# Down-projection of a hybrid layer: weight and product blocks prepared three steps ahead instead of two

## The chip, the cores and the metric

The kernel runs on one core of one Trainium2 chip. The core has a matrix engine (TensorE, PE in the profile; its weight loads are PEld), VectorE (DVE), ScalarE (ACT), GpSimd (POOL), SyncE (SP, used here to issue transfers) and 16 DMA engines. Each engine runs its own instructions in the order in which they stand; between engines, semaphores order the work. The metric is the device time of one execution in microseconds (us); lower is better.

## The reference, cut to what matters

The program is one layer of a streaming encoder: a gated recurrent branch and an attention branch, merged, and then a feed-forward part with a causal convolution. The change lies in the last matrix product, the down-projection.

```python
# x: (1, 512, 1024), D_FF = 3072
...
    h = rms_norm(x, ffn_norm_pre[layer])
    up = jnp.einsum("bsd,df->bsf", h, w_up[layer])
    up = causal_dwconv(up, conv_f_w[layer], conv_f_b[layer])
    gate, val = jnp.split(up, 2, axis=-1)
    ffn_out = jnp.einsum("bsf,fd->bsd", jax.nn.gelu(gate) * val, w_down[layer])
    x = x + rms_norm(ffn_out, ffn_norm_post[layer])
```

Below, y is `gelu(gate) * val` (512 x 3072) and W the matrix `w_down` (3072 x 1024).

## The kernel before

**Seven products in 42 steps.** y is halved by tokens and by the contraction, W by the contraction and by output columns, and the product is formed by Strassen's scheme in Winograd's form: seven products of 256 tokens x 1536 x 512 columns instead of eight, in the order `PRODUCTS = (1, 4, 5, 6, 7, 3, 2)`. Each product runs over six blocks of 256 rows of W, and one block of one product is a step: steps 0 to 5 are product 1, 6 to 11 product 4, 12 to 17 product 5, 18 to 23 product 6, 24 to 29 product 7, 30 to 35 product 3, 36 to 41 product 2. The sums of the parts of W that products 4 to 7 need were formed in DRAM much earlier (the tiles `td`).

**Three matmuls for one.** Every float32 operand is split into a rounded high part and the rest: `Split.hi` (L205, ScalarE) writes `wh` from the fetched `raw` weights, `Split.lo` (L208, VectorE) writes `wl = raw - wh`. `y_hi` (L1461, ScalarE) and `y_lo` (L357, VectorE) do the same with a block of y, into `ah` and `al`. `down_step(i)` then issues twelve matmuls (L1495 to L1497: high by high, high by low, low by high, for two token tiles and two halves of the block). `prep(i)` issues the four splitting instructions of step i, in the order wh, ah (ScalarE), wl, al (VectorE). `load_w(i)` issues the fetch of `raw` on SyncE's queue.

**Buffers.** `raw`, `wh` and `wl` have four buffers each. `ah` and `al` have three for the first six steps and four from step 6 on. A buffer is written again when its last reader is done, and the program's semaphores see to that.

**The order** in this part is that in which the code is written; no scheduler moves it. The loop over steps i from 3 on issued: the fetch of the weights of step i + 5, the matmuls of step i, `prep(i + 2)`, and then a list `extra[i]` of other work:

- loads of blocks of y from DRAM into tiles `q` (L1569, SyncE): the blocks of product 4 in `extra[4..6]`, of product 5 in `extra[6..11]`, of products 6 and 7 in `extra[12..17]`, of products 3 and 2 in `extra[19..24]`, and the gain `gpost` in `extra[5]`
- combinations of such blocks on VectorE (L357 and L1572 with `q` on both sides), which make the blocks of products 5, 6, 7 and 3: the one that makes the block of step j stands in `extra[j - 4]`, for steps 12 to 35
- "holds" on ScalarE (L1600), two copies each that save a sum out of its PSUM bank: product 1 in `extra[6]`, product 4 in `extra[12]`, product 5 in `extra[18]`, and products 1 + 6 in `extra[23]`. Products 6 and 7 are added onto the bank of product 1, so step 24 writes into a bank that the last of these holds reads
- in `extra[9]` the negation of half of the gain and the load of another activation table (L1645, L1646, ScalarE)
- from `extra[30]` on folds of sums into the held ones (L1603, VectorE), multiplications by the gain (L1613, VectorE), sums of squares (L1610, ScalarE), and, in `extra[34]` and `extra[38]`, the root of the mean square of an output tile (L1619 and L272 on VectorE, L270 on ScalarE) with its scaling (L1629, ScalarE)

The last four steps (`LATE`) are issued after the loop, token tile by token tile, so that the first tile of outputs is complete early; the second is formed in two halves of 256 columns. Then come the last folds (L1688), the last root and the outputs.

Of the kernel before, what the change touches and what calls it, by code (L numbers as in the profile page):

```python
# [97 lines left out]
def kernel(  # L98
# [55 lines left out]
    def down_block(i, c, m):  # L154
        return w_down[(2 * i + c) * NS + m]
# [859 lines left out]
    with ExitStack() as at:  # L1015
# [141 lines left out]
        i = KD - 2  # L1157
# [287 lines left out]
    STEPS = [(n, m) for n in PRODUCTS for m in range(NS)]  # L1445
    wd, yraw, yhl, dpools, LATE = {}, {}, {}, [], 4

    def load_w(i):
        if i < len(STEPS):
            n, m = STEPS[i]  # L1450
            wd[i] = Split(td[WQ[n]][m] if n > 3 else down_block(*WQ[n], m), (2, DH), f"dn{n}_{m}")
# [5 lines left out]
    def y_hi(i):  # L1457
        pl, b = (ypool, 3) if i < NS else (dpools[0], LATE)
        yhl[i] = [pl.tile([P, 2, SH], F32R, tag=f"a{x}", name=f"a{x}{i}", bufs=b) for x in "hl"]
        yhl[i].append(yraw[STEPS[i]])  # L1460
        act.copy(yhl[i][0], yhl[i][2])  # L1461

    def y_lo(i):
        sub(yhl[i][1], yhl[i][2], yhl[i][0].bitcast(F32))

    def prep(i):
        if i < len(STEPS):
            wd[i].hi()
            y_hi(i)
            wd[i].lo(dve)  # L1470
            y_lo(i)
# [3 lines left out]
    def down_step(i, ts=(0, 1), c=None):  # L1475
        n, m = STEPS[i]
        fresh = n in (1, 2, 4, 5)
        if m == 0 and fresh and ts[0] == 0:
            slot[n] = [bank(f"dn{n}_{t}") for t in range(2)]
            if n == 2:  # L1480
                slot[n][1] = [slot[n][1], bank("dn2_2")]
        dst = slot[{6: 1, 7: 1, 3: 5}.get(n, n)]
        wh, wl = wd[i].parts()
        ah, al = yhl[i][:2]
        for t in ts:
            tok = slice(P * t, P * (t + 1))
            outs = [(dst[t], slice(0, DH))]
            if isinstance(dst[t], list):
                outs = [(dst[t][h], x) for h, x in enumerate((X, Y)) if c in (None, x)]
            for d, x in outs:  # L1490
                h = slice(x.start // 2, x.stop // 2)
                for k in range(2):
                    first, last = fresh and m == k == 0, m == NS - 1 and k == 1
                    bh, bl = turns(wh[:, k], SH)[:, h], turns(wl[:, k], SH)[:, h]
                    pe.matmul(d[:, x], ah[:, k, tok], bh, start=first, stop=False, skip_group_check=True)  # L1495
                    pe.matmul(d[:, x], ah[:, k, tok], bl, start=False, stop=False, skip_group_check=True)  # L1496
                    pe.matmul(d[:, x], al[:, k, tok], bh, start=False, stop=last, skip_group_check=True)  # L1497
# [13 lines left out]
    with man2:  # L1511
# [152 lines left out]
            extra[a].append(lambda t=t: (square(t, 1, kept[6][t]), gained(t, 1, kept[6][t])))  # L1664

        for i in range(3, len(STEPS)):
            load_w(i + 5)
            if i < len(STEPS) - LATE:
                down_step(i)
            if i < len(STEPS) - LATE:  # L1670
                prep(i + 2)
                for f in extra[i]:
                    f()
        for i in range(len(STEPS) - LATE, len(STEPS)):
            prep(i + 2)
        for i in range(len(STEPS) - LATE, len(STEPS)):
            for f in extra[i]:
                f()
# [117 lines left out]
```

## Time and profile before

| what | time |
|---|---|
| three runs, median (lowest to highest) | 883.2 us (882.61 to 883.78) |
| the profiled execution's own time | 883.07 us |
| its span, first to last instruction | 881.3 us |
| busy in the span: TensorE, VectorE, ScalarE, GpSimd | 867.8, 738.7, 600.1, 235.8 us |
| first matmul of step 0, last matmul | 760.87, 873.27 us |

The span is shorter than the execution's own time because start and end of the program lie around it. Busy times overlap between engines, so they don't add up. A row of a timeline gives the start and the length of an instruction in us, its engine and line, what it writes and reads, and in brackets how long the engine stood idle before it and what ended that. A row of the waits view gives an engine's line, what it waited for, and the total, the number and the longest of these waits. Starts count from the span's start, and an engine may start an instruction a little before the one before it has ended.

### The profile page before, as it was taken

Reading aid. Unit: us, or ns where it says so; the run is one execution under the profiler, and the core shown is the slowest. Engines: PE = TensorE matmul, PEld = TensorE weight load, DVE = VectorE, ACT = ScalarE, POOL = GpSimd, SP = SyncE. Lnnn points to the kernel's source line nnn. Section 1 sums busy time; section 2 is a strip of 40 time slices with the busy share of each in tenths; the row PEclk is TensorE's granted clock in tenths of the full one; section 3 lists DMA queues with packets and bytes.
Section 4 is the critical chain, followed back from the end, with each engine's and each line's share of the span. In section 5 each row is a group of like instructions: output and inputs, shape, how many; then the busy total and the mean of one; then the engine's idle time right before and its main releaser. Section 6 shows DMA issues by size and latency. Waiting matters only on the chain.

```text
span 881.3 us, 15793 instructions
## 1 busy us (share of the span) xinstructions
PE 867.8 (98%) x5856; PEld 792.9 (90%) x5856; DVE 738.7 (84%) x1209; ACT 600.1 (68%) x1031; POOL 235.8 (27%) x283
## 2 busy tenths in 40 slices
PE   9999999999999999999999999999999999999996
PEld 7888888888899998888888889999999999988885
DVE  8986479738878849998968698999999999889897
ACT  7565695533466648786755487878888888677664
POOL 4244334535411024223204100233233333100000
PEclk9999999999999999999999999999999999999998
DMA  7788689999864478344506663689999998699875
GB/s 269 235 264 234 193 195 267 250 270 189 193 176 140 120 259 276 136 164 136 203 26 201 221 203 105 147 207 248 257 239 249 235 215 215 221 388 349 296 204 156
DMA packets 71968, 188.38 MB, mean 214 GB/s; under 512 B 7313, under 2 KB 27841, under 8 KB 71506
## 3 DMA queue, kind: packets, MB, share of 16 engines
q1 hardware_dynamic: 48288, 130.86, 44.7%
q0 software_dynamic: 23456, 56.37, 29.7%
q8 instruction: 46, 0.75, 0.3%
q14 instruction: 32, 0.26, 0.1%
q10 hardware_dynamic: 146, 0.14, 0.1%
HBM read 152.79 MB, written 37.83 MB: 216 GB/s over the span
## 4 chain that ended last, share of the span: by engine, by line
PE 82%; DVE 8%; issue 4%; ACT 2%; POOL 2%; DMA 1%; DVEq 0%; SPq 0%; ACTq 0%; POOLq 0%
PE up L462 7%; PE up L464 7%; PE up L461 7%; PE dn L1497 2%; PE ga L252 2%; PE ga L251 2%; PE ga L253 2%; PE dn L1496 2%; PE dn L1495 2%; PE pb L251 2%; PE xa L251 2%; PE v L341 2%; PE xa L253 2%; PE v L342 2%; PE v L343 2%
## 5 line engine op out<-in xcount | busy, mean ns | idle before, releaser
L397 POOL DMA_DIRECT2D ml<-raw_up x42 | 36.1, 860 | 149.6 <-ACT ml L396 84.2
L1370 DVE SCALAR_TENSOR_TENSOR u<-up,cpt,u 128x511 f32<-128x511 f32 x96 | 71.3, 745 | 3.5 <-ACT u L1364 1.8
L1497 PE MATMUL dn<-wh_dn,al 128*128 128x512 f32 (+1 forms) x180 | 66.2, 368 | 0.4
L1496 PE MATMUL dn<-wl_dn,ah 128*128 128x512 f32 (+1 forms) x180 | 65.9, 366 | 0.0
L1495 PE MATMUL dn<-wh_dn,ah 128*128 128x512 f32 (+1 forms) x180 | 65.7, 365 | 0.0
L461 PE MATMUL up<-sh,th 128*128 128x256 f32 x252 | 59.5, 275 | 0.0
L462 PE MATMUL up<-sl,th 128*128 128x256 f32 x252 | 59.5, 275 | 0.0
L208 DVE TENSOR_TENSOR wl_dn<-raw_dn,wh_dn 128x1024 fp32r<-128x1024 f32 x42 | 51.2, 1220 | 7.3 <-ACT wh_dn L205 7.3
L205 ACT CAST wh_dn<-raw_dn 128x1024 fp32r<-128x1024 f32 x42 | 44.0, 1049 | 15.6 <-PE dn L1497 8.3
L357 DVE TENSOR_TENSOR tl<-t,th 128x1024 fp32r<-128x1024 f32 x42 | 51.1, 1217 | 0.0
L1364 ACT ACTIVATE u<-up,cpt 128x512 f32<-128x512 f32 x48 | 36.9, 777 | 20.1 <-PE up L464 10.0
L461 PEld LDWEIGHTS up<-sh,th 128*128 128x128 f32 x252 | 48.4, 192 | 0.0
L462 PEld LDWEIGHTS up<-sl,th 128*128 128x128 f32 x252 | 48.4, 192 | 0.0
L1378 POOL TENSOR_TENSOR yf<-u,u 128x512 f32<-128x512 f32 x23 | 30.5, 1325 | 57.6 <-issue 44.7
L443 ACT CAST th<-t 128x1024 fp32r<-128x1024 f32 x42 | 43.7, 1044 | 2.4
L1497 PEld LDWEIGHTS dn<-wh_dn,al 128*128 128x128 f32 x180 | 34.1, 189 | 6.3 <-DVE al L357 2.2
L461 PE MATMUL up<-h2h,mh 128*128 128x256 f32 x168 | 39.7, 275 | 0.0
L462 PE MATMUL up<-h2l,mh 128*128 128x256 f32 x168 | 39.7, 275 | 0.0
L1050 ACT ACTIVATE P<-P,mx 128x384 f32<-128x384 f32 (+3 forms) x64 | 35.2, 552 | 5.6 <-DVE mx L1045 4.6
L955 POOL TENSOR_TENSOR B<-B,mask 128x128 f32<-128x128 f32 x64 | 29.4, 488 | 34.8 <-DMA B<-cnd 34.7
L464 PE MATMUL up<-sh,tl 128*128 128x256 f32 x252 | 38.4, 275 | 0.0
L1496 PEld LDWEIGHTS dn<-wl_dn,ah 128*128 128x128 f32 x180 | 34.1, 189 | 4.7 <-DVE wl_dn L208 0.6
(731 smaller groups left out, 3234.6 us busy)
## 6 DMA issues: line engine op xcount, KB each, us to landing
raw_up<-in_w_up_dram SPq DMA_DIRECT2D x48, 512.0 KB, 5.6
td<-in_w_down_dram POOLq DMA_DIRECT2D x36, 512.0 KB, 6.6
raw_dn<-td SPq DMA_DIRECT2D x24, 512.0 KB, 5.3
ml<-raw_up POOLq DMA_DIRECT2D x21, 512.0 KB, 5.4
B<-cnd POOLq DMA_DIRECT2D x16, 640.0 KB, 5.7
raw_dn<-in_w_down_dram SPq DMA_DIRECT2D x18, 512.0 KB, 4.0
raw_wo<-in_w_out_dram SPq DMA_DIRECT2D x16, 512.0 KB, 4.3
td<-td POOLq DMA_DIRECT2D x12, 512.0 KB, 11.7
```

What stands on the lines that cost most here:

```text
L205: act.copy(self.wh, self.raw)
L208: engine.tensor_tensor(out=self.wl, in0=self.raw, in1=self.wh.bitcast(F32), op=ALU.subtract)
L251: pe.matmul(dst, ah, bh, start=first, stop=False)
L357: dve.tensor_tensor(out=out, in0=a, in1=b, op=ALU.subtract)
L443: act.copy(self.th[i], self.t[i])
L461: pe.matmul(dst, wh[:, k], turns(ah[:, k]), start=first and k == 0, stop=False, skip_group_check=True)
L462: pe.matmul(dst, wh[:, k], turns(al[:, k]), start=False, stop=False, skip_group_check=True)
L464: pe.matmul(dst, wl[:, k], turns(ah[:, k]), start=False, stop=k == KH - 1, skip_group_check=True)
L1370: dve.scalar_tensor_tensor(out=c[:, s:], in0=ps[:, : S - s], scalar=col(C_CFW + 3 * e + j), in1=c[:, s:], op0=ALU.mult, op1=ALU.add)
L1495: pe.matmul(d[:, x], ah[:, k, tok], bh, start=first, stop=False, skip_group_check=True)
L1496: pe.matmul(d[:, x], ah[:, k, tok], bl, start=False, stop=False, skip_group_check=True)
L1497: pe.matmul(d[:, x], al[:, k, tok], bh, start=False, stop=last, skip_group_check=True)
```

## The change

The preparation behind step i is that of step i + 3, and the fetch that of step i + 6. The preparation of step 5 and the fetch of step 8 are issued ahead of step 3. Buffers, instructions and the lists `extra` stay as they were, and the loop behind the steps issues what is left.

```diff
         for i in range(3, len(STEPS)):
-            load_w(i + 5)
+            if i == 3:
+                prep(5)
+                load_w(8)
+            load_w(i + 6)
             if i < len(STEPS) - LATE:
                 down_step(i)
-            if i < len(STEPS) - LATE:
-                prep(i + 2)
+                prep(i + 3)
                 for f in extra[i]:
                     f()
         for i in range(len(STEPS) - LATE, len(STEPS)):
-            prep(i + 2)
+            prep(i + 3)
```

How the engines' orders change is shown at three places. In the rows, `wh_dn6_5` is the rounded weight tile of block 5 of product 6 (step 23), `ah25` the rounded product block of step 25, `q11_1` the loaded or combined block that it is made from; the number at the end of a name counts buffers.

ScalarE around the hold of products 1 + 6, before:

```order
L205 CAST wh_dn6_5_9965<-raw_dn6_5_9964 128x1024
L1461 CAST ah23_10059<-q00_5_9962 128x512
L205 CAST wh_dn7_0_9993<-raw_dn7_0_9992 128x1024
L1461 CAST ah24_10084<-q11_0_9569 128x512
L205 CAST wh_dn7_1_10018<-raw_dn7_1_10017 128x1024
L1461 CAST ah25_10109<-q11_1_9571 128x512
L1600 COPY kept6_0_10117<-dn1_0_9452 128x512
L1600 COPY kept6_1_10118<-dn1_1_9453 128x512
L205 CAST wh_dn7_2_10043<-raw_dn7_2_10042 128x1024
L1461 CAST ah26_10138<-q11_2_9573 128x512
```

and now:

```order
L205 CAST wh_dn6_5_9950<-raw_dn6_5_9949 128x1024
L1461 CAST ah23_10044<-q00_5_9972 128x512
L205 CAST wh_dn7_0_9975<-raw_dn7_0_9974 128x1024
L1461 CAST ah24_10069<-q11_0_9569 128x512
L205 CAST wh_dn7_1_10003<-raw_dn7_1_10002 128x1024
L1461 CAST ah25_10094<-q11_1_9571 128x512
L205 CAST wh_dn7_2_10028<-raw_dn7_2_10027 128x1024
L1461 CAST ah26_10119<-q11_2_9573 128x512
L1600 COPY kept6_0_10127<-dn1_0_9452 128x512
L1600 COPY kept6_1_10128<-dn1_1_9453 128x512
```

The two copies of the hold moved behind the casts of step 26. The same happened to the other holds and to the gain.

VectorE at the same place, before (L1572 writes the block of a later step, `q11_2` that of step 26):

```order
L208 TENSOR_TENSOR wl_dn7_0_9994<-raw_dn7_0_9992,wh_dn7_0_9993 128x1024
L357 TENSOR_TENSOR al24_10085<-q11_0_9569,ah24_10084 128x512
L1572 SCALAR_TENSOR_TENSOR q11_2_9573<-q00_2_9887,q11_2_9573 128x512
L208 TENSOR_TENSOR wl_dn7_1_10019<-raw_dn7_1_10017,wh_dn7_1_10018 128x1024
L357 TENSOR_TENSOR al25_10110<-q11_1_9571,ah25_10109 128x512
L1572 SCALAR_TENSOR_TENSOR q11_3_9623<-q00_3_9912,q11_3_9623 128x512
L208 TENSOR_TENSOR wl_dn7_2_10044<-raw_dn7_2_10042,wh_dn7_2_10043 128x1024
```

and now:

```order
L208 TENSOR_TENSOR wl_dn7_0_9976<-raw_dn7_0_9974,wh_dn7_0_9975 128x1024
L357 TENSOR_TENSOR al24_10070<-q11_0_9569,ah24_10069 128x512
L1572 SCALAR_TENSOR_TENSOR q11_1_9571<-q00_1_9871,q11_1_9571 128x512
L208 TENSOR_TENSOR wl_dn7_1_10004<-raw_dn7_1_10002,wh_dn7_1_10003 128x1024
L357 TENSOR_TENSOR al25_10095<-q11_1_9571,ah25_10094 128x512
L1572 SCALAR_TENSOR_TENSOR q11_2_9573<-q00_2_9897,q11_2_9573 128x512
L208 TENSOR_TENSOR wl_dn7_2_10029<-raw_dn7_2_10027,wh_dn7_2_10028 128x1024
```

The combination that makes the block of step 26 stood ahead of the weights of step 25 and stands now right ahead of those of step 26.

SyncE, which issues the transfers, from the fetch of the weights of step 9 (`raw_dn4_3`) on, before:

```order
L199 DMA raw_dn4_3_9601<-td3_3_114 128x1024
L1569 DMA q11_3_9623<-yd9_6583 128x2x256
L199 DMA raw_dn4_4_9625<-td3_4_115 128x1024
L1569 DMA q11_4_9647<-yd10_6584 128x2x256
L1644 DMA gpost_9568<-in_gains_dram 128x1024
L199 DMA raw_dn4_5_9650<-td3_5_116 128x1024
L1569 DMA q10_0_9674<-yd0_6574 128x2x256
L1569 DMA q11_5_9676<-yd11_6585 128x2x256
L199 DMA raw_dn5_0_9682<-td0_0_93 128x1024
```

and now:

```order
L199 DMA raw_dn4_3_9589<-td3_3_114 128x1024
L199 DMA raw_dn4_4_9611<-td3_4_115 128x1024
L1569 DMA q11_3_9633<-yd9_6583 128x2x256
L199 DMA raw_dn4_5_9635<-td3_5_116 128x1024
L1569 DMA q11_4_9657<-yd10_6584 128x2x256
L1644 DMA gpost_9568<-in_gains_dram 128x1024
L199 DMA raw_dn5_0_9660<-td0_0_93 128x1024
L1569 DMA q10_0_9684<-yd0_6574 128x2x256
L1569 DMA q11_5_9686<-yd11_6585 128x2x256
```

Each load of a product block moved behind one more fetch of weights: the block of step 11 (`q11_5`) stood ahead of the weights of step 12 (`raw_dn5_0`) and stands now behind them.

## The prediction

> **What bounds the kernel now.** I read the page first (span, chain), then the windows of the last 110 us, then each engine's timeline there. I call the 42 steps of the down-projection 0 to 41; "weights j" and "block j" are the weight and product block of step j, wh/ah their rounded and wl/al their remaining parts.
>
> ```profile
> span 881.3 us, 15793 instructions
> PE 82%; DVE 8%; issue 4%; ACT 2%; POOL 2%; DMA 1%; DVEq 0%; SPq 0%; ACTq 0%; POOLq 0%
> 820.00:825.00 5.00, 5.00 (x25) 4.38 (x24) 4.88 (x7) 2.16 (x3) 0.00 (x0) 1.00 1.03 356
> 870.00:875.00 5.00, 3.55 (x32) 3.35 (x31) 4.43 (x11) 2.08 (x8) 0.00 (x1) 1.00 0.61 105
> 875.00:881.30 6.30, 0.00 (x0) 0.00 (x0) 2.26 (x6) 0.65 (x3) 0.00 (x0) 0.61 0.67 250
> PEld dn L1497 <- DVE al L357: 2.2, 5, 0.5
> PEld dn L1496 <- DVE wl_dn L208: 0.6, 2, 0.4
> ```
>
> The first number of a windows row is the stretch, then the busy time of PE, PEld, DVE, ACT, POOL, the granted clock, the DMA share and GB/s. TensorE is never idle from 820 to 825, and all its waits of the whole stage come to 2.2 + 0.6 = 2.8 us, always for VectorE's subtractions. So a deeper preparation could win at most 2.8 us while TensorE stays the bound.
>
> ```profile
> 822.46 1.22 DVE L208 TENSOR_TENSOR wl_dn<-raw_dn,wh_dn 128x1024 fp32r<-128x1024 f32 x1
> 823.60 0.68 DVE L357 TENSOR_TENSOR al<-q,ah 128x512 fp32r<-128x512 f32 x1
> 824.20 0.68 DVE L1572 SCALAR_TENSOR_TENSOR q<-q,q 128x512 f32<-128x512 f32 x1
> 827.14 1.22 DVE L208 TENSOR_TENSOR wl_dn<-raw_dn,wh_dn 128x1024 fp32r<-128x1024 f32 x1 [2.26 <-ACT wh_dn L205]
> ...
> 844.12 1.22 DVE L208 TENSOR_TENSOR wl_dn<-raw_dn,wh_dn 128x1024 fp32r<-128x1024 f32 x1
> ...
> 853.47 0.22 DVE L1619 TENSOR_SCALAR ss_o<-s_o 128x1 f32<-128x1 f32 x1
> ...
> 856.42 1.23 DVE L208 TENSOR_TENSOR wl_dn<-raw_dn,wh_dn 128x1024 fp32r<-128x1024 f32 x1 [1.62 <-ACT wh_dn L205]
> ...
> 865.18 1.22 DVE L208 TENSOR_TENSOR wl_dn<-raw_dn,wh_dn 128x1024 fp32r<-128x1024 f32 x1
> ...
> 874.40 0.42 DVE L1688 TENSOR_TENSOR kept<-dn,kept 128x256 f32<-128x256 f32 x1
> ```
>
> These are wl25, al25, one combination of product blocks (call it s), wl26, wl33, the sum of squares of output tile 2, wl37, wl41, and the last fold. A step costs VectorE 1.14 (wl to al) + 0.60 (al to s) + 0.60 (s to wl) = 2.34 us.
>
> ```profile
> 825.37 0.38 PE L1495 MATMUL dn<-wh_dn,ah 128*128 128x512 f32 x1
> ...
> 827.96 0.38 PE L1495 MATMUL dn<-wh_dn,ah 128*128 128x512 f32 x1
> ...
> 873.27 0.28 PE L1497 MATMUL dn<-wh_dn,al 128*128 128x256 f32 x1
> ```
>
> Steps 24 and 25 begin here: a step is 2.59 us on TensorE. VectorE is thus a little faster than TensorE until folds join it; the sums of the last token half end at 873.27 + 0.28 = 873.55, but their fold starts at 874.40, because VectorE is behind. **The end hangs on VectorE**, which from wl37 (856.42) on stops only for three short square-root round trips.
>
> **The change part by part.** (a) No instruction is added or removed. The waits are on the same buffers: four of each weight tile, so wh of step j may be written when step j-4 has run, and raw weights j are fetched when wl of step j-4 is done. The preparation of step 5 ahead of step 3, and the late loop, leave ScalarE's and VectorE's order as it was: 0 us. What moves is what stands between the preparations, shown in the rows of the change: holds, the gain's scaling, the combinations s and the loads of product blocks all come one preparation later.
>
> (b) SyncE: block loads now stand behind one more weight load.
>
> ```profile
> 777.08 0.32 SPq L199 DMA_DIRECT2D raw_dn<-td  x1
> 777.45 0.53 SPq L1569 DMA_DIRECT2D q<-yd  x1
> ...
> 781.04 0.32 SPq L199 DMA_DIRECT2D raw_dn<-td  x1
> ...
> raw_dn<-td SPq DMA_DIRECT2D x24, 512.0 KB, 5.3
> raw_dn<-in_w_down_dram SPq DMA_DIRECT2D x18, 512.0 KB, 4.0
> 780.00:785.00 5.00, 4.99 (x23) 4.07 (x22) 4.65 (x6) 5.00 (x8) 0.00 (x0) 1.00 1.05 397
> ```
>
> ```profile
> 780.18 1.05 ACT L205 CAST wh_dn<-raw_dn 128x1024 fp32r<-128x1024 f32 x1
> 781.13 0.62 ACT L1461 CAST ah<-q 128x512 fp32r<-128x512 f32 x1
> 781.65 1.06 ACT L1600 COPY kept<-dn 128x512 f32<-128x512 f32 x2
> 782.61 1.06 ACT L205 CAST wh_dn<-raw_dn 128x1024 fp32r<-128x1024 f32 x1
> ...
> 786.95 1.04 ACT L205 CAST wh_dn<-raw_dn 128x1024 fp32r<-128x1024 f32 x1 [1.30 <-DMA raw_dn<-td]
> 788.41 0.62 ACT L1461 CAST ah<-q 128x512 fp32r<-128x512 f32 x1 [0.42 <-DMA q<-yd]
> 788.94 0.62 ACT L1645 ACTIVATE gpost<-gpost 128x512 f32<-128x512 f32 x1
> ...
> 790.98 1.03 ACT L205 CAST wh_dn<-raw_dn 128x1024 fp32r<-128x1024 f32 x1
> ...
> 803.91 0.62 ACT L1461 CAST ah<-q 128x512 fp32r<-128x512 f32 x1 [0.26 <-DVE q L1572]
> ...
> 820.44 1.06 ACT L205 CAST wh_dn<-raw_dn 128x1024 fp32r<-128x1024 f32 x1 [1.01 <-PE dn L1497]
> ...
> 824.28 0.59 ACT L1600 COPY kept<-dn 128x512 f32<-128x512 f32 x1 [2.27 <-PE dn L1497]
> 825.57 0.59 ACT L1600 COPY kept<-dn 128x512 f32<-128x512 f32 x1 [0.71 <-PE dn L1497]
> 826.06 1.05 ACT L205 CAST wh_dn<-raw_dn 128x1024 fp32r<-128x1024 f32 x1
> ```
>
> At 788.41 ScalarE rounds block 11 (ah11) as soon as its load has landed, so that lands at 788.3. The DMA engines are full then (share 1.05, 397 GB/s) and what SyncE issues lands in its order. The load of block 11 now stands behind weights 12 as well: 524 KB at 397 GB/s, 1.3 us, gives 789.6. To that comes a pause: block 9 and weights 10 are issued by 777.98, and the next, weights 11, waits as before for wl7 until 781.04. Weights 11 landed at 786.85 (wh11, 786.95) behind block 10 and the gain as well, which now come later (786 KB, 2.0 us); in an unbroken stream they would land at 784.85, with the page's medians at 785.0 (4.0, little traffic) or 786.3 (5.3). The pause thus costs 0.2 to 1.5. Bounds of block 11's landing: 788.3 (nothing lost) and 791.1; I take **789.9**, near the row of little traffic, since the pipe is almost empty there.
>
> (c) ScalarE and VectorE are now coupled. Before, s for block j+1 stood ahead of wl of step j, a whole step early; now s for block j stands right ahead of wl j, and ah j waits for it. Prices from the rows: s to ah is 0.77 (803.14 to 803.91, below), ah to the next cast 0.52 (781.13 to 781.65), wh to wl 1.08 (826.06 to 827.14), two hold copies 0.96 (781.65 to 782.61), gain with its table load 2.04 (788.94 to 790.98).
>
> ```profile
> 803.14 0.68 DVE L1572 SCALAR_TENSOR_TENSOR q<-q,q 128x512 f32<-128x512 f32 x1
> ```
>
> From s, a chain of s, ah, wh, wl takes 0.77 + 0.52 + 1.08 = 2.37 us against VectorE's own 0.60 + 2.34 = 2.94: a slack of 0.57. Two hold copies put in between (0.96) now stop VectorE for 0.39, and the gain (2.04) for 1.47. Walk from the landing L of block 11: ah11 L + 0.07, al11 + 0.64 = 0.71 (ah takes 0.62), s12 + 0.60 = 1.31, ah12 + 0.77 = 2.08, gain + 0.52 = 2.60, wh13 + 2.04 = 4.64, wl13 + 1.08 = 5.72. Twelve steps of 2.34 and the two holds of products 4 and 5 (0.39 each) bring wl25 to 5.72 + 28.08 + 0.78 = 34.58; al25 35.72, s26 36.32, ah26 37.09. TensorE waits little on the way: al13 is done at L + 7.55 = 797.4, and its step 13, eleven steps of 2.59 before step 24, wants it at 825.37 - 28.49 + 0.43 = 797.31.
>
> (d) **The step that decides**: the hold of products 1 + 6 (824.28 and 825.57 before, as soon as step 23 ends). Step 24 adds to the same bank, so its first matmul waits for the first hold copy. Now ah26 stands ahead of that copy on ScalarE, and ah26 waits for s26. The copy starts at L + 37.09 + 0.52 = 37.61, ends 0.59 later, and step 24 starts at L + 38.2 = 828.1 instead of 825.37: **TensorE stops 2.75 us**. Queued behind the copy on ScalarE are wh27 and all after it; behind step 24, the release of its buffers.
>
> (e) The end. After the stop wh j waits for TensorE again: 820.44 is wh25, 0.25 after step 22's start (825.37 - 5.18 = 820.19), so wl j starts 0.25 + 1.08 = 1.33 after the start of step j-3. Step 30 starts at 828.1 + 6 x 2.59 = 843.6, wl33 at 845.0 (before 844.12). From there VectorE is slower than TensorE: two steps of 2.94 (an s and a fold or gain), two of 2.34 to wl37, 1.74 to the sum of squares, 2.95 from that to wl38 (853.47 to 856.42, the root and scaling on ScalarE, one step later than now), three of 2.34: 22.25, so wl41 at 867.25 against 865.18. From wl41 on the order is the old one and VectorE is the bound, so the end moves by the same **+2.1 us**. TensorE's end moves by at most its stop, to 873.55 + 2.75 = 876.3, still ahead of the last fold at 874.40 + 2.1 = 876.5.
>
> The profiled execution took 883.07 us (span 881.3, 1.8 around it), 0.13 under the median 883.2, far within the runs' 882.61 to 883.78. Sum: 883.07 + 2.1 = **885.2 us**.
>
> **The rivals.**
> *Not slower: the idle time at 824.88 goes.* Before, wh26 stood behind the hold and VectorE idled 2.26 us before wl26; now wh26 stands ahead. If VectorE comes in no later than before (wl25 by 821.8), s26 starts by 823.5, the hold copy ends by 825.37 and TensorE never stops. Then wl33 is at its earliest, 1.33 after step 30's start at 840.9, so 842.2; + 22.25 = 864.5, 0.7 earlier than 865.18: 882.4. For it: today's wl25 is at 822.46, and one combination (0.6) less will stand ahead of it. Against it: the later landing, the gain and the two holds, by which (b) and (c) put wl25 at 824.5. It turns at that 821.8; each 1 us later costs 1 us. Chance 0.1, and 0.26 for a stop between 0 and 2.4 us (882.4 to 884.8).
> *The clock falls.* The matmuls end at 873.55 and the mean clock of the last 6.3 us is 0.61; if it falls to one half, it stayed full for 1.4 us of them, to 876.4: 2.85 us without matmuls were enough. A stop of 2.75 us or more could do the same. If it then stays low for as long as it took to fall, TensorE loses another 1.4: 886.6. Against it: the stop forecast is a little shorter than this one instance. Chance 0.12.
> The Trainium skill, page "TensorE: Matmul & The Clock Gate", section "Part 1: The HAM clock gate (the "warmup" mystery)", says the clock halves after an idle window of about 3.4 us, free-running. By that rule a 2.75 us stop alone would not lower it, and the forecast stands; the fall here 2.85 us after the last matmul fits such a window only if a little work in it doesn't save it.
> *Nothing happens*, because the four buffers allow no more lead than before: 883.1, if the coupling in (c) costs nothing. It is against the order of the rows; I count it into the 0.26.
>
> **How the numbers follow.** Forecast 885.2, chance 0.52, itself from 884.4 (landing 789.1) to 886.4 (landing 791.1). With the early end 0.1, the short stop 0.26 and the clock 0.12. The range 882.9 to 887.1 leaves out the early end, part of the shortest stops and the worst of the clock. About 0.2% (1.8 us) is what a measurement can tell from no change. Slower by more: the forecast above 884.97 (0.36), the clock (0.12) and a tenth of the rest: 0.52. Faster by more needs under 881.4, which no case gives: 0.03. Same: 0.45.
>
> **What would show it.** Right: a hold copy waiting behind a cast for the combination before it, and a stop of TensorE of 2 to 3.4 us at step 24 with the waits view naming the hold copy; wl25 near 824.5; wl41 about 2 us later. Wrong: step 24 without a stop (then (c) or the landing is too dear), or TensorE's stops at steps 10 to 13 instead, or an end that does not follow wl41.

## The result, and the profile after

The changed kernel took 887.87 us (median of 7 runs, 886.78 to 891.55) beside 883.78 for the kernel before (7 runs): a ratio of 1.0059, 95% interval 1.005 to 1.0069. The forecast was 885.2 with a range of 882.9 to 887.1: right in direction, 2.7 us too low, outside the range. The profiled execution took 887.68 us (span 885.9), 4.61 more than the profiled one of before.

First the page's span, then windows with the columns of before:

```profile
span 885.9 us, 15794 instructions
780.00:785.00 5.00, 4.97 (x23) 4.07 (x22) 4.03 (x5) 4.20 (x8) 0.00 (x0) 1.00 1.01 320
785.00:790.00 5.00, 5.00 (x25) 4.36 (x25) 2.96 (x3) 1.55 (x3) 0.00 (x0) 1.00 1.01 354
790.00:795.00 5.00, 4.38 (x19) 3.23 (x18) 3.63 (x5) 3.81 (x5) 0.00 (x0) 1.00 0.99 362
820.00:825.00 5.00, 5.00 (x25) 4.38 (x24) 5.00 (x8) 3.23 (x4) 0.00 (x0) 1.00 1.01 349
825.00:830.00 5.00, 2.63 (x13) 1.99 (x12) 5.00 (x7) 3.77 (x6) 0.00 (x0) 1.00 1.03 349
830.00:835.00 5.00, 5.00 (x17) 4.05 (x16) 3.02 (x5) 2.42 (x4) 0.00 (x0) 0.66 0.88 299
```

Before, one of these stretches read:

```profile
825.00:830.00 5.00, 5.00 (x25) 4.38 (x24) 2.86 (x4) 4.43 (x7) 0.00 (x0) 1.00 0.64 201
```

Three things are new. From 825 to 830 TensorE is busy for 2.63 us only. From 830 to 835 it is busy all the time, but at a mean clock of 0.66, and does 17 matmuls where 25 fit. And around 790 there is a smaller gap. The waits view names the engine and line for the largest:

```profile
ACT ah L1461 <- DMA q<-yd: 5.0, 2, 4.2
PE dn L1495 <- ACT kept L1600: 2.4, 1, 2.4
```

TensorE waited 2.4 us in one piece for the hold copy (`kept`, L1600), as the prediction's part (d) said. ScalarE waited 4.2 us in one piece for a product block, where before it waited 0.42 us for the same block. The timelines of the changed kernel show both (TensorE, ScalarE, VectorE):

```profile
764.45 0.48 PE L1497 MATMUL dn<-wh_dn,al 128*128 128x512 f32 x1
...
825.99 0.38 PE L1496 MATMUL dn<-wl_dn,ah 128*128 128x512 f32 x1
826.21 0.38 PE L1497 MATMUL dn<-wh_dn,al 128*128 128x512 f32 x1
828.96 0.48 PE L1495 MATMUL dn<-wh_dn,ah 128*128 128x512 f32 x1 [2.37 <-ACT kept L1600]
...
790.72 0.62 ACT L1461 CAST ah<-q 128x512 fp32r<-128x512 f32 x1 [4.17 <-DMA q<-yd]
...
827.80 0.62 ACT L1461 CAST ah<-q 128x512 fp32r<-128x512 f32 x1 [0.77 <-DVE q L1572]
828.32 1.07 ACT L1600 COPY kept<-dn 128x512 f32<-128x512 f32 x2
...
825.28 1.22 DVE L208 TENSOR_TENSOR wl_dn<-raw_dn,wh_dn 128x1024 fp32r<-128x1024 f32 x1
...
847.62 1.23 DVE L208 TENSOR_TENSOR wl_dn<-raw_dn,wh_dn 128x1024 fp32r<-128x1024 f32 x1 [0.16 <-ACT wh_dn L205]
...
869.88 1.22 DVE L208 TENSOR_TENSOR wl_dn<-raw_dn,wh_dn 128x1024 fp32r<-128x1024 f32 x1
```

The ScalarE rows are ah11, ah26 and the hold; the VectorE rows wl25, wl33 and wl41. The first row is the third matmul of step 1. In the profile of before it starts here:

```profile
765.53 0.48 PE L1497 MATMUL dn<-wh_dn,al 128*128 128x512 f32 x1
```

I use this matmul as a **mark**: what stands ahead of it is the same in all kernels here, and scatters by a microsecond or more from one execution to the next. Counted from the mark, wl41 starts at 105.43 instead of 99.65. So the changed part lost 5.78 us in this execution, and an earlier start gave 1.08 back: 4.7, close to the 4.61 of the whole.

### The profile page after: what moved, and what is told of

Same layout as the page of the kernel before. It is cut to its first block, busy times and chain, and to the rows that moved or that the text cites. A ratio compares the mean times of both kernels' runs of the same rounds, so it can differ in the third digit from the quotient of the medians.

```text
span 885.9 us, 15794 instructions
## 1 busy us (share of the span) xinstructions
PE 870.6 (98%) x5856; PEld 794.3 (90%) x5856; DVE 740.7 (84%) x1209; ACT 599.8 (68%) x1031; POOL 231.2 (26%) x283
## 4 chain that ended last, share of the span: by engine, by line
PE 80%; DVE 10%; issue 3%; ACT 3%; DMA 3%; POOL 0%; SPq 0%; DVEq 0%; ACTq 0%
PE up L462 7%; PE up L461 7%; PE up L464 7%; PE ga L253 2%; PE ga L252 2%; PE ga L251 2%; PE pb L251 2%; PE pa L252 2%; PE pa L251 2%; PE xa L251 2%; PE v L341 2%; PE xa L252 2%; PE v L343 2%; PE pa L253 2%; PE v L342 2%
## 5 line engine op out<-in xcount | busy, mean ns | idle before, releaser
L1495 PEld LDWEIGHTS dn<-wh_dn,ah 128*128 128x128 f32 x180 | 34.5, 192 | 8.0 <-ACT kept L1600 2.8
```

## The experiments

All were timed on one chip, beside the kernel before there (median 882.8 to 883.1 us):

| run | what is in it | median us | ratio to before, 95% |
|---|---|---|---|
| e1_hold_first | changed kernel, hold ahead of step 26's preparation | 886.95 | 1.0042, 1.0028 to 1.0056 |
| e2_extra_first | before, only SyncE's order changed | 885.94 | 1.0024, 1.0011 to 1.0037 |
| e3_loads_first | changed kernel, SyncE's order of before | 884.09 | 1.0018, 1.0006 to 1.003 |
| e4_gain_late | changed kernel, gain loaded later | 884.53 | 1.0027, 1.0016 to 1.0037 |
| e5_again | changed kernel | 888.55 | 1.0069, 1.0051 to 1.0087 |
| e6_both_first | e1 and e3 together | 884.0 | 1.0009, 1.0 to 1.0017 |
| e7_hold_behind_26 | before, only the hold behind step 26's preparation | 881.42 | 0.9984, 0.9975 to 0.9994 |
| e8_root_split | e7, both scalings behind the next casts | 882.12 | 0.9995, 0.9985 to 1.0005 |
| e9_root_split_one | e7, only tile 2's scaling there | 880.64 | 0.9976, 0.9964 to 0.9988 |
| e10_hold_again | e7 once more | 881.38 | 0.9982, 0.9971 to 0.9992 |

What their profiles show, from the mark, in us: the start of the cast ah11 (just behind the landing of block 11), the longest distance between two matmuls' starts and the step behind it, the clock afterwards, and the start of wl41.

| run | mark | ah11 | longest gap, step | clock then | wl41 |
|---|---|---|---|---|---|
| before | 765.53 | 22.88 | 0.60, late steps | full | 99.65 |
| changed | 764.45 | 26.27 | 2.75, step 24 | half for 3.41 | 105.43 |
| e1 | 765.34 | 28.63 | 2.46, step 11 | half for 3.41 | 105.44 |
| e2 | 765.15 | 27.13 | 1.75, step 11 | half for 3.41 | 103.68 |
| e3 | 766.00 | 22.44 | 1.60, step 24 | full | 100.19 |
| e4 | 764.33 | 24.55 | 2.24, step 24 | half for 3.41 | 103.19 |
| e5 | 765.05 | 26.62 | 2.75, step 24 | full | 104.09 |
| e6 | 765.12 | 23.81 | 0.77, late steps | full | 101.11 |
| e7 | 762.83 | 23.21 | 0.60, early steps | full | 98.49 |
| e8 | 764.95 | 23.36 | 0.44, early steps | full | 97.28 |
| e9 | 765.02 | 22.97 | 0.49, early steps | full | 97.57 |
| e10 | 765.25 | 23.63 | 0.57, early steps | full | 98.32 |

**The hold first (e1).**

```diff
-        extra[at_[7] - 1].append(lambda: hold(6, slot[1]))
...
                 down_step(i)
+                if i == at_[7] - 1:
+                    hold(6, slot[1])
                 prep(i + 3)
```

> The hold of products 1 + 6 is issued ahead of the preparation of step 26, as it was before the change; everything else is that of the changed kernel. Theory (TensorE's stop at step 24 comes from the hold standing behind the cast of the combined block, and the clock falls because of the stop): the first copy follows the cast of block 25 and starts near 826.0, step 24 starts within 0.4 us of the end of step 23, no half clock afterwards, wl26 goes back by about 0.6 us, wl41 comes about 3 us earlier: 1.0013 of the kernel before (884.9 us), between 1.0005 and 1.0025. Rival (the late landing of block 11 has made VectorE late anyway, and the stop only shows it): the stop goes, but TensorE then waits for wl or al at later steps, and the time stays within 0.7 us of the changed kernel's 887.9.

```profile
794.64 0.48 PE L1495 MATMUL dn<-wh_dn,ah 128*128 128x512 f32 x1 [2.08 <-ACT ah L1461]
...
829.28 0.59 ACT L1600 COPY kept<-dn 128x512 f32<-128x512 f32 x1
830.58 0.58 ACT L1600 COPY kept<-dn 128x512 f32<-128x512 f32 x1 [0.71 <-PE dn L1497]
...
825.00:830.00 5.00, 5.00 (x25) 4.38 (x24) 5.00 (x8) 3.73 (x5) 0.00 (x0) 1.00 1.01 328
```

The two copies are apart again, the second waiting for TensorE, and TensorE is never idle from 825 to 830: the stop at step 24 is gone, so it did come from the hold's place. But wl41 did not move (105.44 behind the mark against 105.43). Block 11 came later still in this execution, and TensorE paid at step 11 (2.08 us waiting for ah11) what it did not pay at step 24. This execution is the slowest of the six of e1 (888.59 us, median 886.95), so it shows the place of the payment better than its size. By the medians 1.0042 is left of the 1.0059 and 1.0069 of the changed kernel, with intervals that overlap. Neither forecast was met: more is left than the theory allowed, and somewhat less than the rival did. The late landing is the larger part, and the hold's place settles in part where it is paid.

**SyncE's order alone (e2).** `for f in extra[i]: f()` moves ahead of `prep(i + 3)`.

> The list of other work behind step i is issued ahead of the preparation of step i + 3, so that ScalarE and VectorE have exactly the order of before; only SyncE's order is that of the changed kernel (weights one fetch ahead of the block loads). Theory: the block of step 11 lands about 2 us later than before, TensorE stops for 0.5 to 1.2 us at step 11, and the idle 2.26 us that VectorE had at wl26 takes in the rest; no stop at step 24: 1.0011 of the kernel before (884.8 us), between 1.0003 and 1.0018. Rival A (SyncE's order is harmless, all of the loss is in the order on ScalarE and VectorE): within 0.05% of before. Rival B (SyncE's order is the whole loss): 1.005 or more.

```profile
792.95 0.48 PE L1495 MATMUL dn<-wh_dn,ah 128*128 128x512 f32 x1 [1.37 <-ACT ah L1461]
...
791.37:794.79 3.42, 1.93 (x7) 1.10 (x7) 2.98 (x4) 2.49 (x4) 0.00 (x0) 1.00 0.90 311
794.79:798.20 3.41, 3.41 (x10) 2.69 (x9) 2.44 (x4) 3.41 (x6) 0.00 (x0) 0.50 0.71 257
```

ah11 came 4.25 us later than before, TensorE stopped at step 11 and not at step 24. That is the theory, at more than twice its price and beyond its range: I had put the landing 2 us later, and had not expected the clock to fall after so short a stop (PEclk 0.50 in the second window). Rival B falls: 1.0024 is less than half of the changed kernel's loss.

**The other order alone (e3).**

```diff
+            for f in fetch[i]:
+                f()
             load_w(i + 6)
```

`fetch` takes the loads of product blocks and of the gain out of `extra`.

> The loads of product blocks and of the gain are issued ahead of the fetch of the weights of step i + 6, so that SyncE has exactly the order of before; ScalarE and VectorE keep the order of the changed kernel. Theory: block 11 lands as before, about 5.7 + 34.6 us ahead of step 24's release less than now: step 24 starts at landing + 38.2, a stop of about 1.2 us, too short for the clock to fall; no stops at steps 11 and 13: 1.0006 of the kernel before (884.3 us), between 1.0 and 1.0018. Rival (the landing does not matter, the coupling of ScalarE and VectorE alone makes the stop): a stop of over 2 us at step 24 again and 1.004 or more.

```profile
826.95 0.48 PE L1495 MATMUL dn<-wh_dn,ah 128*128 128x512 f32 x1 [1.22 <-ACT kept L1600]
...
785.00:790.00 5.00, 5.00 (x25) 4.38 (x24) 3.71 (x5) 2.28 (x4) 0.00 (x0) 1.00 1.05 379
```

The stop is 1.22 us, as forecast, the clock stays full, and the DMA engines again move 379 GB/s. So SyncE's order alone makes the late landing. In this profile wl41 is 0.54 us later than before; the timing says 0.18%, at the upper edge of the forecast range, with an interval that begins at the expected 0.06%.

**The gain later (e4).**

```diff
-        extra[5].append(lambda: nc.sync.dma_start(gpost, gains[3:4, :].partition_broadcast(P)))
-        extra[9].append(lambda: act.mul(gpost[:, DH:], gpost[:, DH:], -1.0))
+        extra[10].append(lambda: nc.sync.dma_start(gpost, gains[3:4, :].partition_broadcast(P)))
+        extra[14].append(lambda: act.mul(gpost[:, DH:], gpost[:, DH:], -1.0))
```

> In the changed kernel the load of the gain goes from the list behind step 5 to that behind step 10, and its negation from behind step 9 to behind step 14 (the table load stays). Theory: the 3.1 us between the landings of block 10 and of the gain were in front of block 11, which now lands about 2.8 us earlier relative to block 10; step 24 starts as much earlier, the stop falls under 2.1 us and the clock stays full: 1.0007 of the kernel before (884.4 us), between 1.0 and 1.002. Rival (the stream was late because of the pause in issuing, and the gain only took its share of a full pipe, 1.3 us): block 11 comes 1.3 us earlier, the stop shortens by 1.3 us at most and the time is 1.003 to 1.0045 of before.

```profile
826.59 0.48 PE L1495 MATMUL dn<-wh_dn,ah 128*128 128x512 f32 x1 [1.86 <-ACT kept L1600]
...
785.00:790.00 5.00, 5.00 (x25) 4.38 (x24) 3.43 (x4) 2.82 (x5) 0.00 (x0) 1.00 1.03 347
825.00:830.00 5.00, 3.41 (x10) 2.74 (x11) 4.68 (x7) 3.06 (x5) 0.00 (x0) 0.73 1.01 345
```

ah11 came 1.7 us earlier than in the first profile of the changed kernel and the stop shrank to 1.86 us, but the clock fell all the same, so the time lies between the two forecasts. The rate around 785 to 790 stayed at 347 GB/s without the gain in it: the gain's own transfer is not what slows the stream.

**The changed kernel again (e5).**

> The changed kernel once more, on the chip of the experiments. Theory (the queue of SyncE runs empty in the pause and the landing of block 11 scatters by microseconds; TensorE's stops then add up to 2 us or more at steps 11 and 24, and the clock falls when a 3.41 us stretch of the fixed grid that the changes of clock show has TensorE busy for less than about 0.56): 1.0045 to 1.0065 of the kernel before, block 11 landing 3 us or more later than in the profile of before, measured from the third matmul of step 1, and one stretch of half clock. Rival (the fall of the clock in the first profile was a chance of one in eight): no stretch of half clock in this profile, and a median nearer 1.003.

```profile
827.15 0.38 PE L1497 MATMUL dn<-wh_dn,al 128*128 128x512 f32 x1
829.90 0.48 PE L1495 MATMUL dn<-wh_dn,ah 128*128 128x512 f32 x1 [2.37 <-ACT kept L1600]
...
828.28:831.69 3.41, 1.79 (x8) 1.61 (x9) 3.09 (x5) 2.95 (x5) 0.00 (x0) 1.00 1.04 350
831.69:835.10 3.41, 3.41 (x17) 2.98 (x17) 3.22 (x5) 1.71 (x3) 0.00 (x0) 1.00 0.91 308
...
846.87 1.23 DVE L208 TENSOR_TENSOR wl_dn<-raw_dn,wh_dn 128x1024 fp32r<-128x1024 f32 x1 [0.16 <-ACT wh_dn L205]
...
869.14 1.22 DVE L208 TENSOR_TENSOR wl_dn<-raw_dn,wh_dn 128x1024 fp32r<-128x1024 f32 x1
```

The same stop to a hundredth, 2.75 us between two starts, and this time the clock stayed at 1.00. Behind the start of step 24 this profile and the first one of the changed kernel make a pair that differs in the clock, and they price it: wl33 stands 847.62 - 828.96 = 18.66 us behind the start of step 24 there, and 846.87 - 829.90 = 16.97 here. **A fall costs 1.69 us.** Without it wl41 still lost 104.09 - 99.65 = 4.44 us. The part of the theory that asked for a half clock in this profile failed: the stretch of the first window above is busy for 1.79 of 3.41 us, 0.52 by the PE column and so under the 0.56, and the clock stayed full. That the stops add up and the landing is over 3 us late held. The median, 1.0069, came out above the forecast range, and far from the rival's 1.003.

**Both undone (e6).**

> The changed kernel with both undone: loads of product blocks ahead of the weight fetch on SyncE, and the hold of products 1 + 6 ahead of the preparation of step 26. What is left of the change is that combinations, folds, the other holds and the gain's scaling stand one preparation later. Theory: block 11 lands as before, no stop at step 11 or 24, full clock throughout; from wl33 on VectorE needs the 22.25 us of the changed order instead of 21.06: 1.0008 of the kernel before, between 1.0 and 1.0016. Rival (the coupling of ScalarE and VectorE itself costs a stop wherever a hold stands): a stop of over 1 us at step 24 and 1.002 or more.

```profile
843.97 1.22 DVE L208 TENSOR_TENSOR wl_dn<-raw_dn,wh_dn 128x1024 fp32r<-128x1024 f32 x1
...
866.23 1.22 DVE L208 TENSOR_TENSOR wl_dn<-raw_dn,wh_dn 128x1024 fp32r<-128x1024 f32 x1
```

No stop, full clock, 1.0009 measured against 1.0008. From wl33 to wl41 it takes 866.23 - 843.97 = 22.26 us, as in the changed kernel, against 21.06 before: the rest of the change costs 1.2 us at the end, where VectorE is the bound.

**The hold behind step 26, and nothing else (e7, e10).** In the kernel before:

```diff
-                prep(i + 2)
+                if i != at_[7]:
+                    prep(i + 2)
                 for f in extra[i]:
                     f()
+                if i == at_[7] - 1:
+                    prep(i + 3)
+                    hold(6, slot[1])
```

> The kernel before, and in it only the hold of products 1 + 6 goes behind the preparation of step 26, as in the changed kernel; the combinations stay a whole step early. Theory (the hold behind the cast of block 26 hurts only because that block is then still to be combined): the casts of step 26 end by 825, the copies start when step 23 ends as before, no stop, the idle 2.26 us of VectorE at wl26 goes and wl33 comes up to 1.9 us earlier: 0.9988 of the kernel before, between 0.998 and 1.0. Rival (a hold behind those casts stops TensorE in any case): a stop of over 1 us at step 24, 1.001 or more.

> The kernel before with only the hold of products 1 + 6 behind the preparation of step 26, a second time. Theory: again faster, 0.9984 of the kernel before, between 0.9975 and 0.9995, no stop of TensorE at step 24. Rival (the first reading was scatter of the earlier stages): 0.9995 or more.

ScalarE and VectorE in e7, from wh26 on; then wl33:

```profile
820.68 1.06 ACT L205 CAST wh_dn<-raw_dn 128x1024 fp32r<-128x1024 f32 x1 [1.01 <-PE dn L1497]
821.64 0.62 ACT L1461 CAST ah<-q 128x512 fp32r<-128x512 f32 x1
822.16 0.57 ACT L1600 COPY kept<-dn 128x512 f32<-128x512 f32 x1
823.23 0.58 ACT L1600 COPY kept<-dn 128x512 f32<-128x512 f32 x1 [0.49 <-PE dn L1497]
...
822.43 1.22 DVE L208 TENSOR_TENSOR wl_dn<-raw_dn,wh_dn 128x1024 fp32r<-128x1024 f32 x1
...
840.26 1.22 DVE L208 TENSOR_TENSOR wl_dn<-raw_dn,wh_dn 128x1024 fp32r<-128x1024 f32 x1
```

The order on ScalarE is that of the changed kernel at this place, and TensorE does not stop: block 26 had been combined a step earlier, ah26 waits for nothing, and the copies come in time. VectorE's idle 2.26 us ahead of wl26 is gone. wl33 stands 77.43 behind the mark instead of 78.59, wl41 98.49 instead of 99.65: 1.16 us earlier. This profile is the fastest of e7's executions (879.14 us, median 881.42). That of e10, near its median (881.53 beside 881.38), says the same: no stop, wl33 at 77.26 and wl41 at 98.32, 1.33 us earlier. Timed twice, it is faster than before by 0.16% and 0.18%.

**The end (e8, e9).** Both take e7 and split the root from the scaling that follows it. The core of e9:

```diff
+            if t == 0:
+                todo += [lambda: scale_of(2), lambda: finish_by_dma(2, nc.gpsimd)]
+            else:
+                todo.append(lambda: (scale_of(3), finish_by_dma(3, nc.sync)))
```

> As the run with the hold behind step 26 in the kernel before, and the scaling of output tile 2 on ScalarE moves one step behind its root, so that the casts of step 37 stand between them. Theory (VectorE sets the end, and its 1.62 us wait for the weights after the root comes from the scaling ahead of them): the wait falls to 0.5 us or less, and wl41 comes another 1.1 us earlier until TensorE's own end becomes the bound: 0.9982 of the kernel before, between 0.997 and 0.9995. Rival (TensorE's end is the bound already): the same as the run without it, within 0.05%.

> As the run with the split root, but only output tile 2 has its scaling one step behind its root; tile 3 keeps its scaling right behind the root, as in the kernel before. Theory (the split brought wl41 forward, but the later scaling of tile 3 put its two transfers, and behind them on SyncE all the last outputs, at the end): tile 3's accumulating transfer lands before the last folds again, the wait of wl37 stays under 0.5 us, and the time is 0.997 of the kernel before, between 0.996 and 0.9985. Rival (the earlier wl41 is worth nothing because the end does not follow it): 0.9984, as with the hold alone, or more.

VectorE at wl37 and wl38 in e8, and the outputs' issues on SyncE; then VectorE at wl37 and at the last fold, and the same issues, in e9:

```profile
852.70 1.23 DVE L208 TENSOR_TENSOR wl_dn<-raw_dn,wh_dn 128x1024 fp32r<-128x1024 f32 x1 [0.19 <-ACT wh_dn L205]
...
855.81 1.23 DVE L208 TENSOR_TENSOR wl_dn<-raw_dn,wh_dn 128x1024 fp32r<-128x1024 f32 x1 [0.69 <-ACT wh_dn L205]
...
873.01 0.34 SPq L1631 DMA_DIRECT2D out_dram<-o  x1
```

```profile
853.06 1.23 DVE L208 TENSOR_TENSOR wl_dn<-raw_dn,wh_dn 128x1024 fp32r<-128x1024 f32 x1 [0.19 <-ACT wh_dn L205]
...
872.05 0.42 DVE L1694 TENSOR_TENSOR kept<-dn,kept 128x256 f32<-128x256 f32 x1 [0.16 <-PE dn L1497]
...
872.17 0.34 SPq L1631 DMA_DIRECT2D out_dram<-o  x1
```

The 1.62 us ahead of wl37 fell to 0.19 in both, and 0.69 came back at wl38. wl41 stands 97.28 behind the mark in e8 and 97.57 in e9, 1.2 and 0.9 us ahead of e7. e8 gave that back: the output of tile 3 (L1631), and behind it in SyncE's queue all the last outputs, was issued 108.06 behind the mark (at 764.95), no earlier than in e7 (107.90). With tile 3 as before it was issued 107.15 behind it (at 765.02), and e9 has the lowest ratio here: 0.9976, 2.4 us by the medians. In its profile, as in that of e8, the last fold waits for TensorE (0.16 us), so the end has reached TensorE's own end. That tile 3's place explains all of e8's difference is argued from the issues. The intervals of e7, e8, e9 and e10 overlap in part, so that e9 is faster than the hold alone is likely and not shown.

## Why the prediction was wrong in size

**(a), (c), (d): right.** From the landing, 0.07 ahead of the cast at 790.72 as in the prediction, to wl25 it took 34.63 us (forecast 34.58), to ah26 37.15 (37.09), to the hold copy 37.67 (37.61), to step 24 38.31 (38.2). The stop came where and why it was said to come, and e1 and e7 show it from both sides: put ahead, the hold stops nothing at step 24, and put behind, it stops nothing either as long as ah26 need not wait for its combination. It did not decide the time by itself: without it 1.0042 is left (e1). That its size agrees (2.75 us from start to start, and 2.75 forecast) is luck: the landing came 1.8 us later than forecast, and TensorE reached the end of step 23 2.1 us late, which was not forecast. The two nearly cancel in the stop. They do not cancel in the time: step 24 started 64.51 behind the mark instead of 59.84, 4.67 later where 2.75 was forecast.

**(e): right in its second half.** From wl33 to wl41 22.26 us (forecast 22.25), in the changed kernel, in e5 and in e6 alike. From step 24 to wl33 16.87 was forecast and 16.97 measured where the clock was full.

**(b): the term that was mis-sized.** "The pause thus costs 0.2 to 1.5 … I take 789.9, near the row of little traffic, since the pipe is almost empty there." That put the landing 1.6 us later than before; ah11 came 3.39 us later from the mark (3.74 in e5, 4.25 and 5.75 in e2 and e1). Counted from the mark of before, that is a landing at 791.7, beyond the upper bound of 791.1 too. Most of the error lies in the rate. I let the stream run on at 397 GB/s and added the pause. It ran at 320 and 354 GB/s (windows 780 to 790), with the DMA share still at 1.01: the engines counted as busy and moved less. With the order of before (e3) it was 379 GB/s again. The second of these windows, before:

```profile
785.00:790.00 5.00, 5.00 (x25) 4.37 (x24) 4.65 (x6) 3.28 (x6) 0.00 (x0) 1.00 1.06 383
```

In 10 us that is (397 + 383 - 320 - 354) x 5 = 530 KB less, 1.4 us at the rate of before, of the 1.8 us by which the landing was later than forecast. "TensorE waits little on the way" fell with it: up to step 24, TensorE was already 2.1 us late by stops at steps 11 and 13 (826.21 + 0.22 - 764.45 = 61.98 from the mark, against 59.84 for step 24 before).

**The clock: a rival with a chance far too small.** I gave 0.12 to a fall, because in the one instance at hand, the end of the program, 2.85 us without matmuls had been needed and the forecast stop was a little shorter. That instance says when the clock fell, not how little would have been enough. Four of the six profiles with a stop of over 1.5 us between two starts have a half clock behind it, after gaps from 1.75 us on (e3 with 1.60 and e5 with 2.75 have none). The price was also a little low: 1.69 instead of 1.4.

The sum for the first profile: forecast 2.1, landing 3.39 - 1.6 = 1.8 more, the clock 1.7: 5.6 of the 5.78 measured from the mark. For e5, without the clock: 2.1 + 3.74 - 1.6 = 4.2 of 4.44.

**The rival on the other side** ("the idle time at 824.88 goes") did not happen in the changed kernel, but its mechanism is real: e7 is that rival, made true by leaving the combinations a step early. It was worth 1.16 us at wl41 (1.33 in e10) and 0.7 in my estimate, where two errors met: I had wl33 come 1.9 us earlier, and it came 1.16 earlier, and I had charged the slower order of the last steps, which e7 does not have.

**Still open**: why the stream runs slower after the pause. SyncE's order is the cause (e2 against e3), and the gain's transfer isn't (e4). In the order of before, two more loads (block 10 and the gain) were issued ahead of the pause, so more was under way when issuing began again; that a fuller queue is what keeps the rate up was not tried by itself. In half-microsecond windows of the changed kernel the loss is a passing dip: 225 to 295 GB/s from 783.5 to 786.0, and 350 or more again from 786.5 to the landing, where the kernel before is never under 330 (776 to 792).

## What to carry to other kernels

A deeper lead moves everything that rides on the loop, not just the preparation: here the combinations, holds and loads kept their place in the list and so lost one step of their own lead, which cost more than the preparation could win. Move one thing at a time: the hold alone was worth 0.16 to 0.18%, and with one scaling moved off the path 0.24%. On an in-order engine, a copy that frees a bank must not stand behind an instruction whose input is still to be made; whether it stands earlier or later matters less.

## What the runs showed of the hardware that I had not expected

The clock falls, and comes back, only at the borders of a fixed grid of 3.41 us: in the first profile of the changed kernel at 830.15 and 833.56, and at the program's end at 881.35, 15 x 3.413 after the first of these. In e1, e2 and e4 the fall at the program's end comes 88.75, 85.33 and 51.20 us behind the first fall: 26, 25 and 15 times 3.413. The windows on that grid, in the first profile of the changed kernel:

```profile
826.74:830.15 3.41, 1.20 (x6) 1.06 (x7) 3.31 (x5) 2.64 (x5) 0.00 (x0) 1.00 1.03 353
830.15:833.56 3.41, 3.41 (x10) 2.65 (x9) 2.43 (x3) 0.88 (x3) 0.00 (x0) 0.50 0.94 302
833.56:836.97 3.41, 3.41 (x17) 3.01 (x16) 2.43 (x3) 2.19 (x3) 0.00 (x0) 1.00 0.38 136
```

PEclk is 1.00 through the window that holds the stop, 0.50 through the next, and 1.00 again. Where the grid lies differs from execution to execution. I added up TensorE's idle time in each window, as every distance between two matmuls' starts less the 0.216 us of one at full clock (the mean of the unbroken rows; 825.99 to 826.21 above): 2.53 (e1), 2.32 (changed), 2.25 (e2) and 2.13 us (e4) were followed by half clock; 1.80 and 1.72 (both e5) and 1.38 (e3) were not. The border thus lies between 1.80 and 2.13 us of 3.41, and a stop of 2.5 us leaves the clock full only when the grid cuts it in two, as it did in e5 (0.91 and 1.72). The ends of the programs agree, though they were not used for this: from the end of the last matmul (0.11 us for one of 256 columns, the distance of the rows there) to the next border, 2.14 us pass in e5, and the clock falls at that border; 1.72 us pass in e1 and 1.43 in e10, and it falls one border later. The PE column does not rank the windows so (1.93 us busy in e2, which fell, and 1.79 in e5, which did not), because the row of a matmul lasts longer than 0.216 us and so covers a part of the gap behind it.

The Trainium skill, page "TensorE: Matmul & The Clock Gate", section "Part 1: The HAM clock gate (the "warmup" mystery)", gives a free-running window of 3413 ns; the traces agree with the length and with its running free. It speaks of an idle window; here a window 2.13 us idle, with matmuls in it (e4), was enough. The prediction's sentence that by that rule a stop of 2.75 us alone would not lower the clock does not hold: it did so in one of two profiles.
